# The state-space layer of a decoder trunk laid out by (set, state), with real and imaginary parts apart

## The chip, the cores and the metric

The kernel runs on one core of a Trainium2 chip. The metric is device time in microseconds (us), from one launch to its end. The kernel before took 1573.6 us (median of three runs, 1571.99 to 1575.98).

## The reference

A decoder trunk over one sequence of 512 tokens and 1024 channels: one S5 state-space layer, one layer of dilated attention, and a squared-ReLU MLP after each. The change is inside the state-space layer alone. That layer cuts the channels into 64 groups of 16; each group has 64 complex states:

```
lam_bar = exp(lam * dt)                                  # 64 groups x 64 states
b_bar   = ((lam_bar - 1) / lam)[..., None] * (b_re + i b_im)   # x 16 channels
bu      = einsum('bsgc,gpc->bsgp', u, b_bar)
state_t = lam_bar * state_(t-1) + bu_t                   # along the 512 tokens
y       = Re(einsum('bsgp,gcp->bsgc', state, c_re + i c_im)) + d * u
z       = gelu(y);  val, gate = split(z @ w_glu);  h += ada_gate * val * sigmoid(gate)
```

Everything after the layer (its GLU, the first MLP, attention, the second MLP, the final norm) is unchanged.

## The kernel before, in words

The 512 tokens are cut into 64 chunks of 8 (L = 8). Inside a chunk the recurrence is a small Toeplitz matrix per group; across chunks it is a scan over 64 steps. The groups form two sets of 32 (s = 0 and 1), and the work runs in four units (ft = 0 to 3), each with 8 groups of either set. For one unit:

- `ssm_p` (VectorE, or GpSimd for some parts): P, the input matrix of the chunk, as two products and one add (L562, L563, L564), each on 128 x 1024 elements for one set. Its argument s is the half of the unit. `ssm_p_tr` turns P with TensorE, one transpose for a group and set (L575), and ScalarE copies the result (L576). Half a unit is 8 transposes.
- `ssm_q` (GpSimd): Q, the output matrix, by three operations for each set (L590 to L592), then b_bar of the unit in its six small operations (L601 to L603, written into `bz`), then `dk`, the skip term, in two (L607).
- `ssm_k` (TensorE): the Toeplitz kernel from `bz`, Q and `dk` (L623, L626, L629); `ssm_k_copy` spreads it on ScalarE into `mt` in 16 copies (L642).
- `ssm_in_tr`/`ssm_in`: turned and modulated input; `ssm_d` (TensorE, L665): the chunk inputs; `ssm_scan` (VectorE; for the last unit the second part of it on GpSimd): rotation (L681 to L687), two scans (L690), rotation back (L700, L701) and the adds that write S (L704), four of 64 partitions because real and imaginary part lie on different partition halves than the scan's rows.
- `ssm_out` (TensorE): Toeplitz part (L718) and state part (L722); `ssm_out_tr` turns the result, applies gelu (L741), and splits it for the GLU (L744, L749).

Before the units, `ssm_params` makes the parameters: B and C arrive by DMA with the groups on partitions, TensorE turns them (L468), ScalarE copies them out in pieces with signs (L473 to L480), so that real part and imaginary part are stacked over the two halves of the partitions, for all 64 groups. `ssm_powers` turns six small matrices (L493) and builds the powers of lam_bar on VectorE and GpSimd (`cmul`, L352 to L357), each operation over 64 groups.

The order of everything in the layer is written out by hand in `ssm()`, and `pinned` keeps that order on TensorE, ScalarE, VectorE and GpSimd: each engine takes its instructions strictly in program order. Other work lies between the units: the dot products of the conditioning vector with `ada_w` (`ada_dot`, L282; `ada_steps`, L1564), whose pieces pass through the tiles `uz` and `h`, so that a piece is fetched when the dot product before has freed its tile; and `transpose_x` (L226 with ScalarE's copies L229). The GLU follows; its weights are fetched, rounded on ScalarE (L799) and their remainder made on VectorE (L801), both held by hand behind the last `ssm_k_copy` and the last scan. From there TensorE's products (L827 to L829) fill the engine. SBUF tiles of the layer come from one pool of 13 (`W`).

Of the kernel before, what the change touches and what calls it, by code (L numbers as in the profile page):

```python
# [11 lines left out]
AF = mybir.ActivationFunctionType  # L12
# [44 lines left out]
def _constants():  # L57
# [37 lines left out]
class Trunk:  # L95
# [29 lines left out]
    def setup(self):  # L125
# [4 lines left out]
        self.ones = self.cst[:, C_ONE:C_ONE + P]  # L130
# [251 lines left out]
    def ssm_params(self):  # L382
# [31 lines left out]
        q = qx[0:G, 0:12].rearrange("p (i j) n -> p i j n", j=2)  # L414
# [9 lines left out]
        nc.scalar.activation(R8, two(RD), AF.Exp, scale=float(L))  # L424
# [13 lines left out]
        v.tensor_scalar(Y8, two(X0), 4.0 / math.pi, None, ALU.mult)  # L438
# [7 lines left out]
        v.tensor_tensor(LR, two(RR), two(C0), ALU.mult)  # L446
        v.tensor_tensor(LI, two(RR), two(S0), ALU.mult)

        l1, l2 = LR[:, 0], LI[:, 0]
# [4 lines left out]
        v.tensor_tensor(CR, two(X1), two(X2), ALU.mult)  # L454
# [3 lines left out]
        v.tensor_tensor(CI, two(X1), two(X2), ALU.mult)  # L458


        bc = [self.w([P, 2, G, 16]) for _ in range(2)]
        self.bT, self.cT = bc
        for vw, o, sgn in ((bn.rearrange("g i (n c) -> g c (i n)", c=16), bc[0], ((1, 1), (-1, 1))),
                           (cn.rearrange("g c i n -> g c (i n)"), bc[1], ((1, -1), (1, 1)))):
            for hb in range(2):
                pt = self.aux_ps().rearrange("p (c g) -> p c g", g=G)
                for ch in range(8):
                    nc.tensor.transpose(pt[:, ch], vw[:, hb * 8 + ch], self.ident[0:G, 0:G])  # L468
                pv = pt.rearrange("p c g -> p g c")
                for j in range(2):  # L470
                    ov = o[:, j, :, hb * 8:hb * 8 + 8]
                    if j == 0 and sgn[j] == (1, 1):
                        nc.scalar.copy(ov, pv)  # L473
                        continue
                    for i in range(2):
                        od, pd = ov[i * 64:i * 64 + 64], pv[(i ^ j) * 64:(i ^ j) * 64 + 64]
                        if sgn[j][i] == 1:
                            nc.scalar.copy(od, pd)
                        else:
                            nc.scalar.mul(od, pd, -1.0)  # L480
        self.dn = dn
        self.q, self.qx = q, qx

    def ssm_powers(self):
# [4 lines left out]
        G = 64  # L489
        q, qx = self.q, self.qx  # L490
        pt = self.aux_ps().rearrange("p (i g) -> p i g", g=G)
        for i in range(6):
            nc.tensor.transpose(pt[:, i], q[:, i].rearrange("g s n -> g (s n)"), self.ident[0:G, 0:G])  # L493
        pw = self.w([P, 4, 8, G])
        pwr, pwi, pcr, pci = [pw[:, i] for i in range(4)]
        t1, t2, t3, t4 = [qx[:, 16 + 4 * i:20 + 4 * i] for i in range(4)]
# [7 lines left out]
        for s in range(2):  # L504
            rows = slice(s * 64, s * 64 + 64)
            v.tensor_copy(rq[rows], pt[rows, 2:4, s * GI:(s + 1) * GI])
# [12 lines left out]
        self.pw = (pwr, pwi, pcr, pci, pc0[:, 0], pc0[:, 1])  # L519
# [21 lines left out]
    def pw4(self, i, ft, s, n):  # L541
        g = s * GI + ft * 8
        return self.pw[i][:, 0:n, g:g + 8].rearrange("p l g -> p g l").unsqueeze(3).broadcast_to([P, 8, n, 16])

    def ch4(self, x, i, ft, s, n):
        g = s * GI + ft * 8
        return x[:, i, g:g + 8].unsqueeze(2).broadcast_to([P, 8, n, 16])
# [6 lines left out]
    def ssm_p(self, ft, s, eng, eng2=None):  # L554

        u = self.unit[ft]
        tz = u["zs"][:, 2 * s:2 * s + 2].rearrange("p i g c -> p (i g c)").rearrange("p (g l c) -> p g l c", g=8, c=16)
        for eng, g in ((eng, slice(0, 5)), (eng2, slice(5, 8))) if eng2 else ((eng, slice(0, 8)),):
            pp, tp = u["pp"][:, s * 8 + g.start:s * 8 + g.stop], tz[:, g]
            pr, pi, b1, b2 = [x[:, g] for x in (self.pw4(2, ft, s, 8), self.pw4(3, ft, s, 8),  # L560
                                               self.ch4(self.bT, 0, ft, s, 8), self.ch4(self.bT, 1, ft, s, 8))]
            eng.tensor_tensor(pp, pr, b1, ALU.mult)  # L562
            eng.tensor_tensor(tp, pi, b2, ALU.mult)  # L563
            eng.tensor_tensor(pp, pp, tp, ALU.add)  # L564

    def ssm_p_tr(self, ft, s):
# [5 lines left out]
        for hb in (2 * s, 2 * s + 1):  # L572
            pt = self.aux_ps().rearrange("p (g x) -> p g x", g=4)
            for j in range(4):
                nc.tensor.transpose(pt[:, j], u["pp"][:, hb * 4 + j].rearrange("p l c -> p (l c)"), self.ident)  # L575
            nc.scalar.copy(u["pT"][:, hb * 4:hb * 4 + 4], pt)  # L576

    def ssm_q(self, ft, eng):
# [6 lines left out]
        for s in range(2):  # L585
            g = s * GI + ft * 8
            g8 = slice(s * 8, s * 8 + 8)
            qs = q[:, g8, 1:8]
            tq = fl[:, 0:896].rearrange("p (g l c) -> p g l c", g=8, c=16)
            eng.tensor_tensor(qs, self.pw4(0, ft, s, 7), self.ch4(self.cT, 0, ft, s, 7), ALU.mult)  # L590
            eng.tensor_tensor(tq, self.pw4(1, ft, s, 7), self.ch4(self.cT, 1, ft, s, 7), ALU.mult)
            eng.tensor_tensor(qs, qs, tq, ALU.subtract)  # L592

        bz = u["bz"] = self.bz[ft % 2]
        for s in range(2):
            g = s * GI + ft * 8
            g8 = slice(s * 8, s * 8 + 8)
            b8 = bz[:, 0:512].rearrange("p (g x) -> p g x", x=32)[:, g8, 16:32]
            tb = fl[:, 896:1024].rearrange("p (g c) -> p g c", c=16)
            c0 = [self.pw[4 + i][:, g:g + 8].unsqueeze(2).broadcast_to([P, 8, 16]) for i in range(2)]  # L600
            eng.tensor_tensor(b8, c0[0], self.bT[:, 0, g:g + 8], ALU.mult)  # L601
            eng.tensor_tensor(tb, c0[1], self.bT[:, 1, g:g + 8], ALU.mult)
            eng.tensor_tensor(b8, b8, tb, ALU.add)  # L603
        dk = u["dk"] = self.t([32, 16, 32], "rstd", 2)
        for s in range(2):
            g = s * GI + ft * 8
            eng.tensor_tensor(dk[:, s * 8:s * 8 + 8], self.dT[:, g:g + 8].unsqueeze(2).broadcast_to([32, 8, 32]),  # L607
                              self.cst[0:32, C_DK:C_DK + 32].unsqueeze(1).broadcast_to([32, 8, 32]), ALU.mult)

    def ssm_k(self, ft):  # L610
# [1159 lines left out]
```

## Time and profile before

| what | value |
|---|---|
| median of three runs | 1573.6 us (1571.99 to 1575.98) |
| profiled execution, its own time | 1572.7 us |
| span of the profiled execution, first to last instruction | 1570.9 us |
| TensorE / VectorE / ScalarE / GpSimd busy | 1468.5 / 945.9 / 569.4 / 134.1 us |
| mean granted TensorE clock, share of full | 0.977 |

A busy time is the union of an engine's instructions. In a view in order of time, a row is a run of instructions of one line: the second number is the time from the start of the first to the end of the last, so neighbouring rows of TensorE overlap by its pipeline. In the chain of waits, rows follow each other without gaps. The text in brackets at the end of a row is idle time just before it and what ended it.

### The profile page before, as it was taken

Reading aid. Unit: us, or ns where it says so; the run is one execution under the profiler, and the core shown is the slowest. Engines: PE = TensorE matmul, PEld = TensorE weight load, DVE = VectorE, ACT = ScalarE, POOL = GpSimd, SP = SyncE. Lnnn points to the kernel's source line nnn. Section 1 sums busy time; section 2 is a strip of 40 time slices with the busy share of each in tenths; the row PEclk is TensorE's granted clock in tenths of the full one; section 3 lists DMA queues with packets and bytes.
Section 4 is the critical chain, followed back from the end, with each engine's and each line's share of the span. In section 5 each row is a group of like instructions: output and inputs, shape, how many; then the busy total and the mean of one; then the engine's idle time right before and its main releaser. Section 6 shows DMA issues by size and latency. Waiting matters only on the chain.

```text
span 1570.9 us, 27064 instructions
## 1 busy us (share of the span) xinstructions
PE 1468.5 (93%) x11540; PEld 1228.3 (78%) x11540; DVE 945.9 (60%) x1641; ACT 569.4 (36%) x989; POOL 134.1 (9%) x112
## 2 busy tenths in 40 slices
PE   2566999999999999979999999999999999999998
PEld 1445789888888888967887888798878888888887
DVE  8989996889874345657774433433558544344322
ACT  5656633424242334421332322332345423232222
POOL 8867100000000001000000000000000000000000
PEclk9888999999999999998999999999999999999999
DMA  9413581976743232354643212221325232332301
GB/s 228 133 55 82 167 236 29 323 230 196 231 143 104 85 121 88 104 164 145 180 141 102 82 55 81 82 82 55 102 84 167 78 111 82 106 99 89 107 1 54
DMA packets 214488, 188.59 MB, mean 120 GB/s; under 512 B 7480, under 2 KB 208352, under 8 KB 214368
## 3 DMA queue, kind: packets, MB, share of 16 engines
q1 hardware_dynamic: 214368, 186.87, 39.2%
q8 instruction: 90, 1.47, 0.4%
q14 instruction: 30, 0.25, 0.0%
HBM read 182.66 MB, written 4.19 MB: 119 GB/s over the span
## 4 chain that ended last, share of the span: by engine, by line
PE 73%; DVE 15%; DMA 7%; issue 3%; ACT 1%; SPq 1%; POOL 0%; DVEq 0%; ACTq 0%
PE mm L827 21%; PE mm L829 20%; PE mm L828 20%; DMA h<-in_ada_w_dram 3%; DVE aacc L1487 2%; DVE W L801 2%; DMA W<-in_attn_w_q_dram 2%; PE mm L1253 1%; PE mm L1254 1%; PE mm L1255 1%; DMA W<-in_mlp_w_dram 1%; PE mm L1170 1%; ACT W L799 1%; PE aux L1142 1%; PE aux L1107 1%
## 5 line engine op out<-in xcount | busy, mean ns | idle before, releaser
L799 ACT CAST W<-W 128x1024 fp32r<-128x1024 f32 (+1 forms) x228 | 223.4, 1030 | 400.2 <-PE mm L828 195.6
L827 PE MATMUL mm<-uz,W 128*128 128x512 f32 (+1 forms) x952 | 360.7, 381 | 3.6 <-DVE h L1383 2.7
L829 PE MATMUL mm<-uz,W 128*128 128x512 f32 (+1 forms) x952 | 358.9, 377 | 3.1 <-DVE W L801 3.1
L801 DVE TENSOR_TENSOR W<-W,W 128x1024 fp32r<-128x1024 f32 (+1 forms) x228 | 265.6, 1196 | 159.1 <-ACT W L799 137.2
L828 PE MATMUL mm<-uz,W 128*128 128x512 f32 (+1 forms) x952 | 358.3, 377 | 2.7 <-DVE uz L749 2.4
L827 PE MATMUL mm<-hid,W 128*128 128x512 f32 (+1 forms) x792 | 300.5, 380 | 0.3 <-ACT hid L1000 0.3
L828 PE MATMUL mm<-hid,W 128*128 128x512 f32 (+1 forms) x792 | 297.4, 376 | 2.5 <-DVE hid L1001 2.5
L829 PE MATMUL mm<-hid,W 128*128 128x512 f32 (+1 forms) x792 | 296.9, 375 | 0.0
L827 PEld LDWEIGHTS mm<-uz,W 128*128 128x128 f32 x952 | 180.2, 190 | 38.0 <-DVE h L1383 2.8
L829 PEld LDWEIGHTS mm<-uz,W 128*128 128x128 f32 x952 | 179.9, 189 | 36.2 <-DVE W L801 3.5
L828 PEld LDWEIGHTS mm<-uz,W 128*128 128x128 f32 x952 | 180.2, 189 | 35.2 <-DVE uz L749 2.8
L828 PEld LDWEIGHTS mm<-hid,W 128*128 128x128 f32 x792 | 150.2, 190 | 29.2 <-DVE hid L1001 3.1
L827 PEld LDWEIGHTS mm<-hid,W 128*128 128x128 f32 x792 | 149.8, 190 | 27.9 <-ACT hid L1000 0.5
L829 PEld LDWEIGHTS mm<-hid,W 128*128 128x128 f32 x792 | 149.9, 189 | 27.2
L852 DVE SCALAR_TENSOR_TENSOR h<-mm,ada,h 128x512 f32<-128x512 f32 (+1 forms) x77 | 54.1, 707 | 146.7 <-PE mm L829 146.6
L1487 DVE SCALAR_TENSOR_TENSOR aacc<-W,cs,aacc 128x256 f32<-128x256 f32 x196 | 95.5, 487 | 4.0
L1126 ACT ACTIVATE sg<-aux,st 128x192 f32<-128x192 f32 (+3 forms) x64 | 36.6, 577 | 154.5 <-DVE st L1124 148.6
L1029 DVE TENSOR_TENSOR sg<-sg 128x512 f32<-128x512 f32 x64 | 43.8, 688 | 55.3 <-ACT uz L1028 55.0
L1027 ACT ACTIVATE sg<-mm 128x512 f32<-128x512 f32 x60 | 35.6, 596 | 112.7 <-PE mm L829 108.5
L1253 PE MATMUL mm<-W,hid 128*128 128x256 f32 x256 | 73.4, 287 | 0.0
L1254 PE MATMUL mm<-W,hid 128*128 128x256 f32 x256 | 72.4, 283 | 0.0
L1255 PE MATMUL mm<-W,hid 128*128 128x256 f32 x256 | 72.4, 283 | 0.0
(329 smaller groups left out, 1699.3 us busy)
## 6 DMA issues: line engine op xcount, KB each, us to landing
W<-in_mlp_w_dram SPq DMA_DIRECT2D x64, 1024.0 KB, 5.4
W<-in_ada_w_dram SPq DMA_DIRECT2D x20, 1024.0 KB, 7.4
h<-in_ada_w_dram SPq DMA_DIRECT2D x64, 256.0 KB, 3.2
W<-in_w_kv_dram SPq DMA_DIRECT2D x12, 1024.0 KB, 5.6
W<-in_w_kv_dram SPq DMA_DIRECT2D x24, 512.0 KB, 4.2
W<-in_attn_w_q_dram SPq DMA_DIRECT2D x24, 512.0 KB, 5.7
W<-in_ssm_w_glu_dram SPq DMA_DIRECT2D x16, 512.0 KB, 5.4
W<-in_kv_ada_w_dram SPq DMA_DIRECT2D x8, 1024.0 KB, 5.6
```

The lines of the kernel that those rows point to most:

```text
L799: h = (nc.gpsimd.tensor_copy if first else nc.scalar.copy)(wh[:, ks], raw[:, ks])
L801: j = eng.tensor_tensor(wl[:, ks], raw[:, ks], wh[:, ks].bitcast(F32), ALU.subtract)
L827: nc.tensor.matmul(o, wh[:, k], uh, start=(start and k == order[0]), stop=False)
L828: nc.tensor.matmul(o, wh[:, k], ul, start=False, stop=False)
L829: self.pe_mark = nc.tensor.matmul(o, wl[:, k], uh, start=False, stop=(stop and k == order[-1])).ins
L852: self.mark = nc.vector.scalar_tensor_tensor(self.h[k][:, cs], src[:, cs], gate[:, k:k + 1], self.h[k][:, cs], ALU.mult, ALU.add).ins
L1029: nc.vector.tensor_tensor(rl, rl, rl, ALU.mult)
L1126: self.act_mark = nc.scalar.activation(p[:, 0:W], ps[:, 0:W], AF.Exp, bias=st[:, 1, e:e + 1], scale=0.125, accum_out=st[:, 2, e:e + 1]).ins
L1253: nc.tensor.matmul(ps[:, j], us[0], wh, start=(k == 0), stop=False)
L1254: nc.tensor.matmul(ps[:, j], us[0], wl, start=False, stop=False)
L1255: nc.tensor.matmul(ps[:, j], us[1], wh, start=False, stop=(k == KT - 1))
L1487: nc.vector.scalar_tensor_tensor(acc, raw[k], self.cs[:, k:k + 1], acc, ALU.mult, ALU.add)
```

## The change

Real and imaginary part are now kept as an index of the free dimension, and the two sets lie on the two halves of the partitions. `pw`, `bT`, `cT`, `pp`, `q` and `S` change their layout accordingly.

- `ssm_params`: B and C are turned part by part by plain float32 products with the identity (`by_set`), one for each channel, part and set, into 32 x 64 corners of the array; four whole copies take the place of fourteen. The parameters are no longer duplicated (`two` is gone).
- `ssm_powers`: operations over 32 groups instead of 64.
- `ssm_b_bar`: b_bar once for all units, six operations of 128 x 512 on GpSimd after the first Q; `ssm_bz` copies a unit's share into `bz` on ScalarE just ahead of `ssm_k`.
- `ssm_p`: the add is dropped; the two terms stay apart, and `ssm_p_tr` turns and adds them by two accumulating products, with the identity or its negative.
- `ssm_k`: products over 64 rows and 32 columns, the parts accumulated; `ssm_out`: state part as two products over 64 rows and 64 columns.
- `ssm_scan`: two adds of 128 partitions instead of four of 64; one scratch tile fewer.
- `dk` in one operation, `ssm_rt`'s copies of C in one; the reciprocal of `rs` ahead of the first P.

```diff
+    def by_set(self, out, x):
+        for s in range(2):
+            rows = slice(s * GI, s * GI + GI)
+            self.nc.tensor.matmul(out[s * 64:s * 64 + 64], x[rows], self.ident[rows, rows], start=True, stop=True,
+                                  tile_position=(s * GI, s * 64))
...
+        bc = self.w([P, 2, 2, GI, 16])
+        self.bT, self.cT = bc[:, 0], bc[:, 1]
+        for t, vw in enumerate((bn.rearrange("g i (n c) -> g c i n", c=16), cn)):
+            for i in range(2):
+                pt = self.aux_ps().rearrange("p (c g) -> p c g", g=GI)
+                for ch in range(16):
+                    self.by_set(pt[:, ch], vw[:, ch, i])
+                ov, pv = bc[:, t, i], pt.rearrange("p c g -> p g c")
+                if t and i:
+                    nc.scalar.mul(ov, pv, -1.0)
+                else:
+                    nc.scalar.copy(ov, pv)
...
+    def ssm_b_bar(self, eng, scratch):
+        tb = scratch[:, 0:512].rearrange("p (g c) -> p g c", c=16)
+        for i, op in enumerate((ALU.subtract, ALU.add)):
+            eng.tensor_tensor(self.bb[:, i], self.pc0[0], self.bT[:, i], ALU.mult)
+            eng.tensor_tensor(tb, self.pc0[1], self.bT[:, 1 - i], ALU.mult)
+            eng.tensor_tensor(self.bb[:, i], self.bb[:, i], tb, op)
...
             eng.tensor_tensor(pp, pr, b1, ALU.mult)
             eng.tensor_tensor(tp, pi, b2, ALU.mult)
-            eng.tensor_tensor(pp, pp, tp, ALU.add)
+        u["tp", i] = tz
...
             for j in range(4):
-                nc.tensor.transpose(pt[:, j], u["pp"][:, hb * 4 + j].rearrange("p l c -> p (l c)"), self.ident)
+                for k, (x, m) in enumerate(((u["pp"][:, hb * 4 + j], self.ident),
+                                            (u["tp", s][:, hb % 2 * 4 + j], self.ident if s else self.neg))):
+                    nc.tensor.matmul(pt[:, j], x.rearrange("p l c -> p (l c)"), m, start=(k == 0), stop=(k == 1))
...
+    def ssm_bz(self, ft):
+        bz = self.unit[ft]["bz"] = self.bz[ft % 2]
+        self.nc.scalar.copy(bz[:, 0:512].rearrange("p (i g x) -> p i g x", i=2, x=32)[:, :, :, 16:32],
+                            self.bb[:, :, ft * 8:ft * 8 + 8])
...
+            for lag in range(2):
+                for i in range(2):
+                    for q_ in (0, 2, 1, 3):
+                        m = i * 8 + j * 2 + q_ % 2
+                        z = 32 * m + (0 if lag else 16)
+                        rows = slice(q_ // 2 * 64, q_ // 2 * 64 + 64)
+                        nc.tensor.matmul(pk[q_ * 32:(q_ + 1) * 32, j, 16 * lag:], bz[rows, z:z + 32],
+                                         q[rows, m, 0:8 - lag].rearrange("p l c -> p (l c)"),
+                                         start=(lag == i == 0), stop=False, tile_position=(q_ // 2 * 64, q_ * 32))
...
-            for s in range(2):
-                rows = slice(s * 64, s * 64 + 64)
-                self.mark = v.tensor_tensor(S[i * 64:i * 64 + 64, :, s, 1:], ta[rows], tb[rows], op).ins
+            self.mark = v.tensor_tensor(ta, ta, tb, op).ins
...
-                for s in range(2):
-                    g = s * 8 + gi
-                    nc.tensor.matmul(py[s * 64:(s + 1) * 64, jj], S[:, gi, s],
-                                     q[:, g].rearrange("p l c -> p (l c)"), start=False, stop=True)
+                for i in range(2):
+                    for s in range(2):
+                        rows = slice(s * 64, s * 64 + 64)
+                        nc.tensor.matmul(py[rows, jj], S[rows, i, gi], q[rows, i * 8 + gi].rearrange("p l c -> p (l c)"),
+                                         start=False, stop=(i == 1), tile_position=(s * 64, s * 64))
...
         self.ssm_q(0, pool)
+        self.ssm_b_bar(pool, self.unit[0]["uu"][:, 1].rearrange("p g x -> p (g x)"))
+        self.nc.vector.reciprocal(self.rs, self.rs)
         self.ssm_p(0, 0, dve)
-        self.nc.vector.reciprocal(self.rs, self.rs)
...
+        self.ssm_bz(0)
         self.ssm_k(0)
...
+        self.ssm_bz(1)
         self.ssm_k(1)
...
         self.ssm_p_tr(3, 1)
         self.unit_mark = self.pe_mark
+        self.ssm_bz(2)
         self.ssm_k(2)
         self.ssm_in(3, (1,))
         self.ssm_rt(3)
         self.ssm_k_copy(2, act)
         end()
         end = self.ssm_out_tr(1)
+        self.ssm_bz(3)
         self.ssm_k(3)
 
         self.ssm_d(3)
         self.ssm_k_copy(3, act)
         self.ssm_out(2)
```

## Rows read from the trace of the kernel before

**Rows 1.** The page's 40 equal slices: busy tenths of TensorE and of VectorE.

```profile
PE   2566999999999999979999999999999999999998
DVE  8989996889874345657774433433558544344322
```

**Rows 2.** The chain of waits: start us, us, engine and line.

```profile
95.17 0.69 DVE W L681
...
154.89 0.60 DVE W L681
...
166.50 0.68 DVE W L704
...
167.30 1.90 DVE W L801 x3
169.24 0.80 PE mm L829
```

**Rows 3.** VectorE in order of time: start us, us, operation, shapes.

```profile
52.50 1.21 DVE L562 TENSOR_TENSOR W<-W,W 128x1024 f32<-128x1024 f32 x1
...
61.61 3.14 DVE L562 TENSOR_TENSOR W<-W,W 128x1024 f32<-128x1024 f32 x1
```

**Rows 4.** GpSimd in order of time.

```profile
54.82 1.79 POOL L590 TENSOR_TENSOR uz<-W,W 128x896 f32<-128x896 f32 x1 [2.37 <-PE aux L282]
...
63.60 2.80 POOL L590 TENSOR_TENSOR uz<-W,W 128x896 f32<-128x896 f32 x1
...
72.14 0.41 POOL L601 TENSOR_TENSOR bz<-W,W 128x128 f32<-128x128 f32 x1
```

**Rows 5.** TensorE in order of time, first half of the layer; "128*64" is the stationary tile.

```profile
11.80 1.97 PE L468 MATMUL aux<-cst,uz 64*128 64x64 f32 x16 [1.24 <-DMA uz<-in_ssm_c_im_dram]
...
67.23 0.85 PE L282 MATMUL aux<-uz,aacc 128*32 128x384 f32 x8 [1.79 <-DMA uz<-in_ada_w_dram]
70.37 3.40 PE L575 MATMUL aux<-cst,W 128*128 128x128 f32 x16 [2.28 <-DVE W L564]
...
84.83 0.74 PE L308 MATMUL aux<-redb,cst 128*128 128x96 f32 x2 [2.41 <-DVE redb L305]
```

**Rows 6.** TensorE in order of time, second half of the layer.

```profile
121.51 1.94 PE L575 MATMUL aux<-cst,W 128*128 128x128 f32 x8 [11.58 <-DVE sqs L653]
...
132.89 0.69 PE L718 MATMUL aux<-W,W 128*64 128x128 f32 x4 [5.89 <-DVE sg L1568]
...
138.58 0.40 PE L718 MATMUL aux<-W,W 128*64 128x128 f32 x4
...
139.12 1.10 PE L575 MATMUL aux<-cst,W 128*128 128x128 f32 x8
...
145.88 0.42 PE L623 MATMUL aux<-uz,bz 128*32 128x128 f32 x8
...
149.24 2.08 PE L665 MATMUL mm<-hid,W 128*64 128x64 f32 x64
```

**Rows 7.** The chain of waits after the layer, at a plain float32 product with 128 stationary columns.

```profile
255.81 0.79 PE aux L956 x8
```

**Rows 8.** TensorE in order of time, in the attention: a change of tile shape.

```profile
1166.78 0.67 PE L1115 MATMUL aux<-W 64*32 64x128 f32 x32
1167.38 0.50 PE L827 MATMUL aux<-uz,W 128*128 128x512 f32 x1
1167.72 0.40 PE L828 MATMUL aux<-uz,W 128*128 128x512 f32 x1
1167.96 0.40 PE L829 MATMUL aux<-uz,W 128*128 128x512 f32 x1
```

**Rows 9.** ScalarE in order of time, around the last two units.

```profile
142.53 2.50 ACT L342 ACTIVATE hid<-mm,mod 128x64 f32<-128x64 f32 x8
...
145.75 6.84 ACT L642 COPY W<-aux 32x512 f32<-32x512 f32 x16
...
154.43 1.19 ACT L744 CAST uz<-W 128x512 fp32r<-128x512 f32 x2
```

More of the change, by code (lines that the diff above doesn't have):

```diff
@@ L129, in setup @@
         self.ident = self.cst[:, C_ID:C_ID + P]
-        self.ones = self.cst[:, C_ONE:C_ONE + P]
+        self.ones = self.cst[:, C_ONE:C_ONE + 1]
+        self.neg = self.cst[:, C_NEG:C_NEG + P]
         self.swap = self.cst[:, C_SWAP:C_SWAP + P]
@@ L457, in ssm_params @@
         v.tensor_tensor(X1, X1, X3, ALU.subtract)
[L458 to L480, printed above, removed]
+        v.tensor_tensor(CI, X1, X2, ALU.mult)
+        bc = self.w([P, 2, 2, GI, 16])
[10 more added lines that the diff above has]
+                    nc.scalar.copy(ov, pv)
         self.dn = dn
         self.q, self.qx = q, qx
+    def by_set(self, out, x):
[3 more added lines that the diff above has]
+                                  tile_position=(s * GI, s * 64))
     def ssm_powers(self):
@@ L488, in ssm_powers @@
         pool = nc.gpsimd
-        G = 64
+        G = GI
         q, qx = self.q, self.qx
-        pt = self.aux_ps().rearrange("p (i g) -> p i g", g=G)
+        pt = self.aux_ps()[:, 0:6 * G].rearrange("p (i g) -> p i g", g=G)
         for i in range(6):
-            nc.tensor.transpose(pt[:, i], q[:, i].rearrange("g s n -> g (s n)"), self.ident[0:G, 0:G])
-        pw = self.w([P, 4, 8, G])
+            self.by_set(pt[:, i], q[:, i])
+        pw = self.w([P, 64, G])
+        self.bb = pw[:, 32:64].rearrange("p x g -> p (x g)").rearrange("p (i g c) -> p i g c", i=2, c=16)
+        pw = pw[:, 0:32].rearrange("p (i l) g -> p i l g", i=4)
         pwr, pwi, pcr, pci = [pw[:, i] for i in range(4)]
-        t1, t2, t3, t4 = [qx[:, 16 + 4 * i:20 + 4 * i] for i in range(4)]
+        t1, t2, t3, t4 = [qx[:, 16 + 4 * i:20 + 4 * i, 0:G] for i in range(4)]
         v.tensor_copy(pwr[:, 0], pt[:, 0])
@@ L518, in ssm_powers @@
             n *= 2
-        self.pw = (pwr, pwi, pcr, pci, pc0[:, 0], pc0[:, 1])
+        self.pw = (pwr, pwi, pcr, pci)
+        self.pc0 = [pc0[:, i].unsqueeze(2).broadcast_to([P, GI, 16]) for i in range(2)]
+    def ssm_b_bar(self, eng, scratch):
[4 more added lines that the diff above has]
+            eng.tensor_tensor(self.bb[:, i], self.bb[:, i], tb, op)
     def ssm_turns(self):
@@ L594, in ssm_q @@
[L594 to L603, printed above, removed]
@@ L604, in ssm_q @@
-        dk = u["dk"] = self.t([32, 16, 32], "rstd", 2)
[L605 to L608, printed above, removed]
+            eng.tensor_tensor(qs, self.pw4(0, ft, 7), self.ch4(self.cT, i, ft, 7), ALU.mult)
+            eng.tensor_tensor(tq, self.pw4(1, ft, 7), self.ch4(self.cT, 1 - i, ft, 7), ALU.mult)
@@ L646, in ssm_rt @@
         nc = self.nc
-        for s in range(2):
-            g = s * GI + ft * 8
-            nc.scalar.copy(self.unit[ft]["q"][:, s * 8:s * 8 + 8, 0], self.cT[:, 0, g:g + 8])
+        nc.scalar.copy(self.unit[ft]["q"].rearrange("p (i g) l c -> p i g l c", i=2)[:, :, :, 0],
+                       self.cT[:, :, ft * 8:ft * 8 + 8])
         rt = self.unit[ft]["rt"] = self.t([P, 8, NC], "sqs")
@@ L698, in ssm_scan @@
             e = eng[i]
-            ta, tb = [self.t([P, 8, NC], "sg" if e is v else "rstd", 2)[:, :, 0:n] for _ in range(2)]
+            ta = S[:, i, :, 1:]
+            tb = self.t([P, 8, NC], "sg" if e is v else "rstd", 2)[:, :, 0:n]
             e.tensor_tensor(ta, wr, a1, ALU.mult)
             e.tensor_tensor(tb, wi, b1, ALU.mult)
-            for s in range(2):
-                rows = slice(s * 64, s * 64 + 64)
-                self.mark = v.tensor_tensor(S[i * 64:i * 64 + 64, :, s, 1:], ta[rows], tb[rows], op).ins
+            self.mark = v.tensor_tensor(ta, ta, tb, op).ins
     def ssm_out(self, ft):
```

85 lines of the change are left out of this document (36 added, 49 removed).

## The prediction, made before the changed kernel was run

> **What bounds the kernel now.** I read the slices first, then the chain of waits, then each engine in order of time. In the slices [rows 1] the layer is the first four, some 160 us: VectorE is at 8 or 9 tenths, TensorE at 2 to 6; from the fifth on TensorE is full. So the layer is where VectorE counts, and what lies behind it moves as a block with the moment at which TensorE fills. The chain [rows 2] names that moment: the last scan starts at 154.89 (L681), its last add (L704) ends near 167.2, three remainders of weights (L801) follow, and at 169.24 TensorE goes on with the GLU. I forecast the shift of 169.24 and add what TensorE does more behind it.
>
> Two things must be seen beside the chain. GpSimd and VectorE hinder each other: a product of VectorE over 128 x 1024 takes 1.21 us at 52.50 and 3.14 at 61.61 [rows 3], and GpSimd's L590 1.79 alone and 2.80 against it [rows 4]; 1.21 + 1.79 is 3.0. They take turns, so in such stretches the sum of both counts. And TensorE already ends waits in places: it waits for a piece of `ada_w` at 67.23 [rows 5], and 1.94 us of transposes at 121.51 come after 11.58 us of idling [rows 6].
>
> **What goes from VectorE and GpSimd.** VectorE at 1.18 ns a column (1.21 us for 1024): P's adds, six of 1024 and one of 640, 8.0 us; the powers, 24 operations of half the width (1536 columns fewer), 1.8; S's adds, eight of sixteen at 0.68 [rows 2], 5.4. Together 15.2. GpSimd at 1.8 ns a column ((1.79 - 0.41) / 768, [rows 4]): 24 operations for b_bar at 0.41, 9.8; its adds in P, 1408 columns, 2.8; powers, 1152 columns, 2.1; half of `dk`, about 0.8. Added: six operations of 512 columns at 1.1 (from 0.41 and 1.79), 6.6, bounded by those two rows at 2.5 and 10.7. Net 8.9 less. If VectorE stayed the bound everywhere, all of it, 24 us, would be won. It doesn't stay.
>
> **Start, up to the first `ada_first` (52.50).** `by_set` needs 64 products for B and 64 for C. A float32 product leaves two records where a transpose leaves one: `ssm_d`'s 32 products are the 64 records of L665, 2.08 us [rows 6], 32 ns each with 64 stationary columns. So 256 records and 24 for the powers are 9.1 us, against 32 transposes in twice 1.97 [rows 5]. B's first ran 3.2 us before 11.80, waiting for DMA; B's real part needn't wait for the imaginary one. The end comes 0 to 3.3 us later; I take 1. Then VectorE does 1.8 + 1.2 less, GpSimd 2.1 + 2.5 + 0.8 + 2.0 less and 6.6 more, which is 3.8 less for the sum if all of it overlaps. I take -2 at 52.50 (bounds -4 and +2).
>
> **Up to the second scan (95.17).** `ssm_p_tr` of the first unit and `ada_dot` follow on TensorE. Its last piece's DMA starts when an earlier dot product frees the tile, so 67.23 moves by the same 2, and the transposes of unit 1, at 70.37 because VectorE's L564 ended then, can start near 66. There they turn from 16 records into 64, each with 128 stationary columns. The price: L956 has such products, 8 records in 0.79 us, 99 ns [rows 7]; the 16 transposes at 70.37 took 3.40, 0.2 each, and those at 139.12, in the midst of other work, some 0.12 [rows 6]: TensorE has a slow and a fast rate, and the slow one stands behind idle time. So 64 records cost 6.3 to 12.8; I take 8 (slow at first). The next fixed work, `transpose_x` paced by ScalarE, ends at 82.4 now, and VectorE is awaited until 84.83 [rows 5]. After: -4.3 + 4.6 = +0.3 on 82.4, with no wait, so L308 is 2.1 earlier. `ssm_k` may take 1 more or less. Second scan: -2.5 (bounds -7 and +3). VectorE's savings of this stretch turn into idle time ahead of L681: TensorE is the bound here.
>
> **Up to the last `ssm_in` (142.53).** From 95.17 to 121.5 VectorE is the bound now. Afterwards it needs about 20 us instead of 26, as GpSimd can't begin unit 3's Q before TensorE has used the last `ada_steps` piece, and TensorE's own row (out(0) + 2, transposes + 2.2, a wait for `bz` of 0.5) reaches the transposes of 121.51 after 20.5. So -2.5 - 5.7 = -8. From there ScalarE leads: transposes in 32 records (3.2), two copies, `mt` in 12 copies; out(1), at 132.89 because it waited for VectorE's L1568, can start 9.8 us after the transposes instead of 11.4: -9.6. Then TensorE again. out(1) took 6.2 us, mostly at the slow rate, and its last 8 records 0.54 at the fast one [rows 6]. Its state part becomes twice as many records, which should run two at a time as row tiles do: L1115's 32 records over 64 rows go in 0.60 us, 19 ns [rows 8]. But its tile shape now changes twice for each group. The first L827 after L1115 takes 0.34 us to the next instead of 0.24 [rows 8], so a change costs 0.1 and an out 1.6 more. I take 6.5 (4 to 9): +0.3. The two halves of P for unit 3 add 2.25 each (0.94 to 3.2), the copy of `bz` 0.6. L342 at 142.53 [rows 9]: -9.6 + 0.3 + 4.5 + 0.6 = -4.2.
>
> The Trainium skill, "TensorEngine Tiling (Array Packing)", section Key Properties, says that changing the tiling mode drains the engine; the 0.10 us in rows 8 agrees. It prices no drain, and without one the sum would be about 2 lower.
>
> **The new wait: `bz` of unit 3.** Now `ssm_k(3)` runs at 145.88 [rows 6], because GpSimd had written `bz` long before. After, `ssm_bz(3)` stands on ScalarE behind `ssm_k_copy(2)` and `ssm_out_tr(1)`. ScalarE has no gap from 142.53 to 155.62 [rows 9], 13.1 us, so `bz` is written 13.5 after L342, and queued behind on TensorE are `ssm_k(3)`, `ssm_d(3)`, out(2), and the scan for `ssm_d(3)`. `ssm_k`, 3.36 now, has 128 records at 19 ns and 32 small ones as now: 3.4 at the fast rate, 6 at the slow; after idling I take 4.7, then 1.3 for the first half of `ssm_d`. The scan starts 19.7 after L342; now it starts 12.4 after (154.89). That is 7.3 lost: -4.2 + 7.3 = +3.1. The scan itself is 1.6 shorter (two adds, less GpSimd): +1.5 at L801. The GLU's own need of ScalarE (L799 behind the last `mt` copy) stands no later than that.
>
> **Sum.** +1.5 at 169.24; behind it, where TensorE is full, out(3) is 2 us longer (8 groups, 16 changes, +1.6 to +3.3): +3.5, less 0.5 for products that fit into TensorE's new gap. +3 on the profiled execution: 1572.7 becomes 1575.7; the median lies 0.9 above that one, so 1576.5. `dk`, `ssm_rt` and ScalarE's fewer copies of parameters cost and bring nothing: ScalarE waits for VectorE's reciprocal there, and that comes earlier only ahead of a wait for P.
>
> **The rivals.**
> - *TensorE stays slow* (slower). Products in short bursts run at the slow rate, 0.2 us a record as at 70.37: unit 1's P +4.8, half of unit 2's +3.2, unit 3's +6.4, out(1) and k(3) +2.8, 17 in all. It decides from about 0.12 a record. For it: the slow rate at 70.37 and 132.89, both after idling. Against: the engine has more to do in between. Taken at a bit over half: 1586.
> - *Stationary load binds at the start* (slower). 16 transposes of 128 columns in 1.97 are 123 ns, 61 for 64 columns. 280 records are then 17.1 us from 8.6 at the latest, ending near 25 instead of 14.4, and all behind moves by 9 more: 1585.5. Against: L665 does 32 ns with 64 columns. The Trainium skill, "TensorE: Matmul & The Clock Gate", section LDWEIGHTS, has the load go by columns alone, at columns / 1.2 ns, 53 for 64, which would make 14.8 us of it, an estimate; L665 disagrees where column halves alternate, and `by_set` alternates them.
> - *Products are cheap* (faster). If a P record costs 54 ns, as L718's and L722's do (0.54 for 8 at 138.58, less the start of the next), the stationary load being hidden: unit 1's P -4.5, unit 2's -1.5, unit 3's -3, outs -3, k(3) -1.3: 1563. Against: L956's 99 ns.
> - *VectorE remains the bound* (faster): all 24 us, 1549.5. For it: it has 9 tenths now. Against: ScalarE's row of 13.1 us ahead of `bz(3)`, which no faster VectorE shortens.
>
> **How the numbers follow.** Chances: forecast 0.46, slow TensorE 0.18, load at the start 0.07, cheap products 0.22, VectorE 0.07. The forecast's own range is 1571 to 1582; the range for all, 1562 to 1587, leaves out VectorE's case and the ends of the others. A measurement tells 0.3% (4.7 us) from no change: below 1568.9 are the two fast cases and a little of the forecast, 0.30; above 1578.3 the two slow ones and a third of the forecast, 0.37; between, 0.33.
>
> **What would show it.** Right: L681's last run near 158, TensorE idle for about 10 us ahead of it, ended by ScalarE's copy of `bz`; 64 records for unit 1's P in about 8 us, and VectorE idle for over 5 us ahead of the second scan; TensorE's GLU going on at about 171. Wrong: P records of 54 or of 200 ns; `ssm_k(3)` not waiting; the first turn of the powers over 3 us late; VectorE without gaps up to 150.

## The result, and the profile after

The changed kernel takes 1597.3 us (median of four runs, 1593.1 to 1604.6), against 1573.2: ratio 1.0156 (95% interval 1.0115 to 1.0196), 24 us more. The forecast was 1576.5, with 1587 as the upper end. The profiled execution is the longest of the four: 1604.6 us, span 1602.8. A second series gave 1597.2 and 1.0155 (1.0136 to 1.0175), so the loss is clear of the noise.

The page's slices, TensorE and VectorE (before: [rows 1]):

```profile
PE   6886989999999999997999999999999999999998
DVE  5976785799885344667665432433457643443422
```

VectorE has come down in the layer, and TensorE has gone up to 6 to 9 tenths from the first slice on. The chain of waits (start us, us, what):

```profile
7.27 12.26 PE aux L476 x221
...
151.34 9.23 issue
...
168.26 0.69 DVE W L679
...
178.77 1.29 DVE W L798 x2
...
202.46 8.44 DMA W<-in_ssm_w_glu_dram
...
280.34 0.79 PE aux L953 x8
```

The last scan (L679, before L681) starts at 168.26 instead of 154.89 [rows 2], the remainders of weights (L798, before L801) at 178.77 instead of 167.30, and L953, which closes the GLU (before L956, 255.81 in [rows 7]), stands 24.5 later. TensorE in order of time:

```profile
63.67 7.41 PE L581 MATMUL aux<-cst,W 128*128 128x128 f32 x64
...
83.89 0.74 PE L308 MATMUL aux<-redb,cst 128*128 128x96 f32 x2 [4.15 <-DVE redb L305]
84.57 1.83 PE L623 MATMUL aux<-uz,bz 64*32 64x128 f32 x32
...
93.37 2.09 PE L663 MATMUL mm<-W,W 128*64 128x64 f32 x64
...
99.64 0.44 PE L714 MATMUL aux<-W,W 128*64 128x128 f32 x4
100.01 0.65 PE L719 MATMUL aux<-uz,W 64*64 64x128 f32 x8
100.59 0.44 PE L714 MATMUL aux<-W,W 128*64 128x128 f32 x4
...
136.39 3.84 PE L581 MATMUL aux<-cst,W 128*128 128x128 f32 x32
...
145.66 1.02 PE L623 MATMUL aux<-uz,bz 64*32 64x128 f32 x32 [0.98 <-ACT bz L606]
...
160.57 1.82 PE L623 MATMUL aux<-uz,bz 64*32 64x128 f32 x32 [9.23 <-issue]
```

The same for a group of `ssm_out` before:

```profile
100.84 0.39 PE L718 MATMUL aux<-W,W 128*64 128x128 f32 x4
...
101.28 0.39 PE L718 MATMUL aux<-W,W 128*64 128x128 f32 x4
```

A group of `ssm_out` lasts 0.95 us from L714 to the next L714, where it lasted 0.44 from L718 to the next; a record of P's sum (L581) takes 113 to 118 ns; a record of `ssm_k` (L623) 30 ns, and 57 behind idling. The loads of the stationary tiles for the same lines (PEld) are:

```profile
7.27 12.23 PEld L476 LDWEIGHTS aux<-cst,uz 32*64 32x64 f32 x222 [3.35 <-DMA uz<-in_ssm_b_re_dram]
...
93.37 1.95 PEld L663 LDWEIGHTS mm<-W,W 128*64 128x64 f32 x64 [0.41 <-issue]
...
100.00 0.41 PEld L719 LDWEIGHTS aux<-uz,W 64*64 64x64 f32 x8 [0.17 <-issue]
...
107.26 3.65 PEld L581 LDWEIGHTS aux<-cst,W 128*128 128x128 f32 x32 [0.17 <-issue]
...
145.66 0.78 PEld L623 LDWEIGHTS aux<-uz,bz 64*32 64x32 f32 x32 [1.17 <-ACT bz L606]
```

A load takes 51 to 55 ns for 64 columns, 114 for 128, 24 for 32; L663 is the exception, 64 columns in 30 ns. P's records go at the pace of their loads: with 128 moving columns, as T, the Toeplitz part of an out (L714), has them too, they take 113 to 118 ns where a record of T takes 54. `by_set` takes 55 ns with only 32 moving columns. For T and S, the state part of an out (L719), it is open whether the load or the 128 moving columns set the 54 ns, since L663 loads T's shape in 30. One reserve on `by_set`: the granted clock is given as 1.00 during it, but also from 37.35 to 43.0, where 30 records of P's sum took 5.88 us, so the level at the start is not sure. VectorE in order of time:

```profile
23.73 0.19 DVE L495 COPY W<-aux 128x32 f32<-128x32 f32 x1 [11.36 <-PE aux L476]
...
94.59 0.69 DVE L679 TENSOR_TENSOR W<-mm,hid 128x512 f32<-128x512 f32 x1 [6.58 <-PE mm L663]
...
168.26 0.69 DVE L679 TENSOR_TENSOR W<-mm,hid 128x512 f32<-128x512 f32 x1 [18.47 <-PE mm L663]
```

Its savings have become waits: 6.6 us ahead of the second scan and 18.5 ahead of the last. The 11.4 at the start are the longer `by_set`. The wait of 18.5 is the forecast new one, as ScalarE in order of time shows:

```profile
145.50 2.48 ACT L342 ACTIVATE hid<-mm,mod 128x64 f32<-128x64 f32 x8
...
150.38 6.83 ACT L641 COPY W<-aux 32x512 f32<-32x512 f32 x16 [1.60 <-PE aux L627]
...
160.06 0.41 ACT L606 COPY bz<-W 128x256 f32<-128x256 f32 x1
```

`bz(3)` (L606) stands behind the copies of `mt` (L641), and TensorE's `ssm_k(3)` starts when it is written.

Two windows, from L342 to the remainders of weights and from there to the GLU's end, give the bill of the second half. Columns: stretch, its length, TensorE's busy time and records, granted clock, DMA share and GB/s. Before:

```profile
142.53:167.30 24.77, 21.25 (x348) 0.93 0.61 171
167.30:255.81 88.51, 86.57 (x471) 0.98 0.61 179
```

After:

```profile
145.50:178.77 33.27, 23.89 (x505) 0.85 0.24 65
178.77:280.34 101.57, 95.69 (x524) 0.98 0.57 166
```

L342 is 3.0 later. The first stretch is 8.5 longer: TensorE idles 9.4 instead of 3.5 and works 2.6 more. The second is 13.1 longer: 9.1 more work, 3.9 more idling. Of the 9.1, out(3) is 4.1 (8 groups, 0.95 against 0.44), and 4.3 are products of the GLU: before, 28 records of L827 to L829 had filled TensorE's gaps ahead of 167.30; after, 9 of L824 to L826 ahead of 178.77; the other 19, each 0.227 after the last, are done behind. The first and the last of the 28 before:

```profile
151.25 0.73 PE L827 MATMUL mm<-uz,W 128*128 128x512 f32 x2
...
165.77 0.39 PE L828 MATMUL mm<-uz,W 128*128 128x512 f32 x1
```

The idling behind 178.77 is three gaps after the change:

```profile
196.44 1.09 PE L735 MATMUL aux<-cst,W 128*128 128x128 f32 x8 [1.36 <-ACT W L721]
...
206.47 0.50 PE L825 MATMUL mm<-uz,W 128*128 128x512 f32 x1 [2.32 <-DVE uz L746]
...
214.95 0.50 PE L824 MATMUL mm<-uz,W 128*128 128x512 f32 x1 [2.20 <-ACT sg L913]
```

The chain of waits runs there, up to 214.95, through the other engines and through the fetch of a GLU weight (202.46), where before it stayed on TensorE from 169.24 on. So the gap at 214.95 goes back to a late weight; whether the other two do is not shown, and no run moves these fetches alone.

### The profile page after: what moved, and what is told of

Same layout as the page of the kernel before. It is cut to its first block, busy times and chain, and to the rows that moved or that the text cites. A ratio compares the mean times of both kernels' runs of the same rounds, so it can differ in the third digit from the quotient of the medians.

```text
span 1602.8 us, 28640 instructions
## 1 busy us (share of the span) xinstructions
PE 1521.8 (95%) x12358; PEld 1272.4 (79%) x12358; DVE 923.5 (58%) x1625; ACT 564.1 (35%) x979; POOL 115.8 (7%) x88
## 4 chain that ended last, share of the span: by engine, by line
PE 79%; DVE 11%; DMA 6%; issue 2%; ACT 1%; SPq 0%; DVEq 0%; ACTq 0%
PE mm L824 21%; PE mm L825 21%; PE mm L826 21%; DMA h<-in_ada_w_dram 3%; DVE aacc L1484 3%; DVE W L798 2%; PE mm L1250 1%; PE mm L1251 1%; PE mm L1252 1%; PE aux L623 1%; DMA W<-in_attn_w_q_dram 1%; PE aux L476 1%; PE aux L581 1%; PE mm L1167 1%; PE aux L1139 1%
## 5 line engine op out<-in xcount | busy, mean ns | idle before, releaser
L824 PE MATMUL mm<-uz,W 128*128 128x512 f32 (+1 forms) x952 | 362.0, 382 | 5.8 <-DVE h L1380 2.7
L826 PE MATMUL mm<-uz,W 128*128 128x512 f32 (+1 forms) x952 | 359.1, 378 | 0.0
L798 DVE TENSOR_TENSOR W<-W,W 128x1024 fp32r<-128x1024 f32 (+1 forms) x228 | 265.5, 1196 | 162.1 <-ACT W L796 139.2
L824 PE MATMUL mm<-hid,W 128*128 128x512 f32 (+1 forms) x792 | 300.4, 380 | 0.3 <-ACT hid L997 0.3
L826 PE MATMUL mm<-hid,W 128*128 128x512 f32 (+1 forms) x792 | 296.8, 375 | 0.0
L824 PEld LDWEIGHTS mm<-uz,W 128*128 128x128 f32 x952 | 180.7, 190 | 40.0 <-DVE h L1380 2.8
L826 PEld LDWEIGHTS mm<-uz,W 128*128 128x128 f32 x952 | 180.5, 190 | 33.0
L824 PEld LDWEIGHTS mm<-hid,W 128*128 128x128 f32 x792 | 150.1, 190 | 28.0 <-ACT hid L997 0.5
L826 PEld LDWEIGHTS mm<-hid,W 128*128 128x128 f32 x792 | 149.9, 189 | 27.1
```

What stands on the lines that cost most here:

```text
L798: j = eng.tensor_tensor(wl[:, ks], raw[:, ks], wh[:, ks].bitcast(F32), ALU.subtract)
L824: nc.tensor.matmul(o, wh[:, k], uh, start=(start and k == order[0]), stop=False)
L826: self.pe_mark = nc.tensor.matmul(o, wl[:, k], uh, start=False, stop=(stop and k == order[-1])).ins
```

## Experiments

Unless it says otherwise, an edit is made on the changed kernel. Ratios are to the kernel before on the same chip, with the 95% interval.

**The wait for `bz(3)`.** `ssm_bz(3)` moved right behind `ssm_bz(2)`, ahead of L342.

```diff
         self.ssm_bz(2)
+        self.ssm_bz(3)
         self.ssm_k(2)
...
-        self.ssm_bz(3)
         self.ssm_k(3)
```

> The changed kernel with one edit: the copy of unit 3's b_bar into bz stands right behind that of unit 2, ahead of ssm_k(2), so that ScalarE's row of mt copies, gelu and casts no longer stands between it and ssm_k(3). My theory (the loss is largely this wait, and b_bar's tile, held until that copy, keeps back the third GLU weight): ssm_k(3) starts right behind the transposes of out(1), near 151.5 instead of 160.6, the last scan's L679 near 158 instead of 168.3, the third weight's DMA goes out 15 us or more earlier than 182.9; the time falls by 9 to 14 us, to 1583 to 1588. Rival (the loss is TensorE's greater number of records, and the wait only covers it): ssm_k(3) moves, but the end moves by under 4 us, to 1593 or more.

1592.3 us, 1.0113 (1.0098 to 1.0129): 5 below the first median, but the two intervals overlap. So both were run again.

> The changed kernel itself once more, beside e1_again on one chip. The first times (1597.3, ratio 1.0116 to 1.0196) and those of e1_bz_early (1592.3, 1.0098 to 1.0129) don't tell from each other by their intervals. Theory (the wait for `bz(3)` costs TensorE 9 us, of which the GLU keeps nearly all): 7 to 10 above e1_again. Rival (most of the wait is given back in the GLU and behind it): 2 to 5 above e1_again.

> The kernel of e1_bz_early once more, beside after_again: 1590 to 1593 by either theory; what tells is the distance between the two.

1597.2 and 1592.9, 1.0119 (1.0101 to 1.0137): 4.3. The windows of e1_again:

```profile
145.67:171.70 26.03, 23.23 (x504) 0.93 0.31 83
171.70:271.70 100.00, 95.82 (x525) 0.98 0.58 169
```

`ssm_k(3)` no longer waits, and the first stretch is 7.2 shorter than in the first profile of the changed kernel; the second is 1.6 shorter: the third GLU weight is fetched from 175.8 on instead of 182.9 (not 15 us earlier, as expected), and TensorE idles 4.2 instead of 5.9. By the stretches from L342 to the GLU's end (134.8, and 132.8 in after_again, against 126.0) the wait costs 7 to 9 us, by the times 4 to 5. In after_again L342 itself came 2.8 earlier than here, half of it because out(1) ran 8.2 us instead of 9.6, more of it at the fast rate; with that the GLU's ends lie 4.0 apart. Whether out(1) runs so by chance, these four profiles don't tell. By the times the rival's size holds, and the theory of 7 to 10 doesn't: the wait is a fifth of the loss.

**P's sum on TensorE.** The adds put back on VectorE and GpSimd, transposes on TensorE; alone, and together with the early `bz`.

```diff
             eng.tensor_tensor(tp, pi, b2, ALU.mult)
-        u["tp", i] = tz
+            eng.tensor_tensor(pp, pp, tp, ALU.add if i else ALU.subtract)
...
-                for k, (x, m) in enumerate(((u["pp"][:, hb * 4 + j], self.ident),
-                                            (u["tp", s][:, hb % 2 * 4 + j], self.ident if s else self.neg))):
-                    nc.tensor.matmul(pt[:, j], x.rearrange("p l c -> p (l c)"), m, start=(k == 0), stop=(k == 1))
+                nc.tensor.transpose(pt[:, j], u["pp"][:, hb * 4 + j].rearrange("p l c -> p (l c)"), self.ident)
```

> The changed kernel with one part undone: P's two terms are subtracted or added by the engine that makes them, and turned by one transpose each. By the records, a half unit goes from 32 records of 118 ns (3.8 us) to 8 (0.95), 2.8 less on TensorE each, and VectorE gets 1.2 to 3 us back for each add. My theory: behind 95 us TensorE and ScalarE lead, so the three half units in the row of units 2 and 3 (2.8 each) come off the end: 7 to 9 us less than the changed kernel, 1588 to 1590, with the wait for bz unchanged. Rival (VectorE leads there too): no gain, or up to 5 us slower.

> Both edits of the two kernels before: bz of unit 3 copied early, P's terms added by the engines. If the two losses lie one behind the other, the gains add: 17 to 22 us less than the changed kernel, 1575 to 1580. If they share one wait, the sum is no more than the larger alone: 1583 to 1588.

Alone 1606.7, 1.0209 (1.0191 to 1.0228), worse than the change; together 1589.1, 1.0100 (1.0080 to 1.0120), 3 below the early `bz` alone, which the intervals don't tell apart. Both miss what I expected. With the adds, L308 comes at 89.9 instead of 83.9: in the first half the sum on TensorE is worth 6 us. In the second it costs: in e12_both the last scan starts at 155.0, as before the change, and the remainders of weights at 167.6, though L308 came 5.7 later than with the early `bz` alone. Yet the GLU ends at 269.4, 13.7 late. So with the wait and P's sum out of the way, the rest of the loss lies behind 167, where I had allowed 1.5: 9.4 us more work of TensorE and 3.9 more idling, as in the changed kernel.

**Price of a change of tile shape.** e12_both, with Toeplitz (T) and state (S) products in the order T S S T, so that one change falls on a group instead of two.

```diff
+                parts = ("t", "s") if jj % 2 == 0 else ("s", "t")
+                for n, part in enumerate(parts):
+                    if part == "t":
...
```

> The kernel with both edits, and in ssm_out the order of Toeplitz and state part turned round for every second group, so that the tile shape changes 8 times in an out instead of 16. Records of the state part are 73 ns each in the changed kernel (0.58 for 8) and the Toeplitz ones 93 (0.37 for 4) where they were 54. If a change of shape costs 0.10 to 0.15, an out falls from 7.6 us by 0.8 to 1.2, and the time by 1 to 3 us against the kernel with both edits. If the records themselves are slow (55 ns for the load of 64 stationary columns), an out stays within 0.3 us of 7.6 and the time doesn't move.

1593.1, 1.0117 (1.0100 to 1.0134): no gain in time: 4 above e12_both, with intervals that overlap. In that run out(1) began late behind VectorE (wait of 4.4 us) and L342 stood 2.9 later than in e12_both. But its rows of TensorE give both prices (L715 is T, L721 S):

```profile
159.97 1.09 PE L721 MATMUL aux<-uz,W 64*64 64x128 f32 x16
160.99 0.66 PE L715 MATMUL aux<-W,hid 128*64 128x128 f32 x8
161.58 1.09 PE L721 MATMUL aux<-uz,W 64*64 64x128 f32 x16
```

Two groups take 1.61 instead of 1.90: a change costs 0.15. S's 16 records take (1.02 - 0.15) / 16 = 54 ns, T's 8 (0.59 - 0.15) / 8 = 55. So a record of S costs as much as one of T: the 64 x 64 tiles on the diagonal of the array gain nothing, where I had counted on two at a time.

**Is TensorE's own time paid in the second half?** The kernel before, with the outs of units 2 and 3 computed twice.

```diff
+                for _ in range(2 if ft > 1 else 1):
...
```

> The kernel before, with the products of `ssm_out` of units 2 and 3 done twice into the same bank (the second time they begin anew, so the sum is the same): 32 records of 54 ns more on each out, 3.5 us, a size like the 4.1 us that the change adds to an out, and nothing else. Theory (from L342 on TensorE is the bound and the GLU's products fill its gaps, so its own work is paid one for one): GLU's end 5.5 to 8 later, 1577 to 1580. Rival (an out lies beside ScalarE's copies and the GLU's products wait for z anyway): GLU's end less than 3 later, 1571 to 1575.

1578.0, 1.0035 (1.0021 to 1.0048): 5.5 us for 7.0 of added records. The window from L342, here 1.0 earlier, to the GLU's end:

```profile
141.57:258.71 117.14, 113.08 (x947) 0.99 0.59 171
```

117.1 us instead of 113.3: 5.2 more work, at a granted clock of 0.99 instead of 0.97, and 1.4 less idling. So in the window 3.9 of the 7.0 are paid. The GLU's end is only 2.9 later, on the rival's side of 3; another 2.6 us of the profiled execution come behind it, where nothing was changed, and only with them does the time reach the theory's range. Added work is paid by more than half, not one for one.

The same question put to the change itself, the split of `ssm_out`'s state part alone in the kernel before (e5_out_halves), has no result. What the outs cost is therefore read from the records and from the windows, and not from a run of its own.

**The start.** e1_bz_early, with C turned behind the factors of the powers.

```diff
         for i in range(6):
             self.by_set(pt[:, i], q[:, i])
+        self.ssm_bc(1)      # C; B alone stays in ssm_params
```

> The changed kernel with `ssm_bz(3)` early (as in e1_bz_early, 1592.3), and C turned behind the powers' factors instead of ahead of them: the 128 records of C leave the path to the first copy of the powers (L495). Theory (the products of `by_set` at 55 ns a record are what delays the start): L495 at 16 instead of 23.6, P's first product near 24 instead of 31.4; of these 7 us the waits for `ada_w` and ScalarE take some, 3 to 7 arrive at the second scan and at the end: 1585 to 1589. Rival (the start is covered by `ada_w`'s transfers): the second scan within 1 of 93.9, 1590 to 1593.

1583.5, 1.0073 (1.0058 to 1.0088), 0.4% less than e1_bz_early, a little more than the theory's best. VectorE in order of time:

```profile
15.82 0.19 DVE L502 COPY W<-aux 128x32 f32<-128x32 f32 x1 [3.45 <-PE aux L482]
...
31.87 0.20 DVE L1600 RECIPROCAL rs<-rs 128x8 f32<-128x8 f32 x1 [8.27 <-ACT rs L208]
```

The copy (L502, L495 before this edit) is 7.8 earlier, but P's first product is not, since the change put the reciprocal of `rs` ahead of it, and that waits for ScalarE. The gain comes later: GpSimd does the first Q from 21.6 on instead of 29.4 and has it out of VectorE's way sooner, the second P is 2.4 earlier and L308 4.8 (78.9).

**P's sum only where TensorE has room.** e6_c_behind with unit 3's P on VectorE; then the order T S S T; then the second half of unit 2 on the engines too.

```diff
+            if ft == 3:                # third run: ft * 2 + i > 4
+                eng.tensor_tensor(pp, pp, tp, ALU.add if i else ALU.subtract)
...
```

> e6_c_behind with the two terms of P of unit 3 alone added on VectorE and turned by transposes; units 0 to 2 stay on TensorE. Theory (TensorE bound from 125 on, VectorE with room there): 5.3 us less for TensorE (64 records at 118 ns against 16 transposes at about 130), 2 to 4 us more for VectorE ahead of the third scan; 3 to 5 us below e6_c_behind. Rival (VectorE or ScalarE ends the stage there): within 1.5 of e6_c_behind or above it.

> e7_p3_on_engines with the two shapes of `ssm_out` in alternating order (Toeplitz, states, states, Toeplitz), which halves the changes of shape. From the trace of e4_out_order a change costs 0.15 us and an out 6.5 instead of 7.6. Theory (TensorE paid one for one): 2 less than e7_p3_on_engines by the last two outs, 1575 to 1578. Rival (ScalarE's copies of y pace the outs, as the 3.2 us wait in e4_out_order says): the same as e7_p3_on_engines or 1 to 2 more.

> e10_order with the second half of unit 2's P added on VectorE and GpSimd too, so that five of eight halves stay on TensorE, as in e11_before_p_5_halves. There the 32 records had run at the slow rate (0.2 us); here TensorE is at work ahead of them and they run at the fast one (0.12), but VectorE waits 3.1 for them all the same (L574 at 112.71). Theory (what counts is the slow rate behind idling): no gain, within 1 of e10_order (1576.8). Rival (what counts is VectorE's wait for the half, at any rate): 2 to 3 less, 1574 to 1575.

1578.5, 1.0044 (1.0027 to 1.0061); 1576.8, 1.0023 (1.0012 to 1.0035); 1579.6, 1.0046 (1.0031 to 1.0061). The first is 4.9 below e6_c_behind, as the theory said. The second lands where its theory put it, but its interval overlaps the first's. The third lies 2.8 above e10_order, where one theory allowed 1 either way and the other wanted a gain; these intervals overlap too, so what holds is that no gain is seen. There I look at VectorE, first in e10_order, then in e13_p_5_halves:

```profile
108.36 1.22 DVE L573 TENSOR_TENSOR W<-W,W 128x1024 f32<-128x1024 f32 x1
112.71 1.36 DVE L574 TENSOR_TENSOR W<-W,W 128x1024 f32<-128x1024 f32 x1 [3.13 <-PE aux L593]
```

```profile
110.03 2.81 DVE L573 TENSOR_TENSOR W<-W,W 128x1024 f32<-128x1024 f32 x1
112.77 2.83 DVE L574 TENSOR_TENSOR W<-W,W 128x1024 f32<-128x1024 f32 x1
```

The wait for the 32 records is gone, but both products now run beside GpSimd's and last 2.8 instead of 1.2 and 1.4: the wait was no loss, since GpSimd worked alone meanwhile (its L607 took 1.80 us in e10_order and 2.79 here).

**The other way round: the kernel before with P's sum on TensorE**, for units 0 to 2, and for the first five halves.

```diff
-            eng.tensor_tensor(pp, pp, tp, ALU.add)
+            if ft == 3:                # second run: ft * 2 + s > 4
+                eng.tensor_tensor(pp, pp, tp, ALU.add)
...
+                for k, x in enumerate((u["pp"][:, hb * 4 + j], u["tp", s][:, hb % 2 * 4 + j])):
+                    nc.tensor.matmul(pt[:, j], x.rearrange("p l c -> p (l c)"), self.ident, start=(k == 0), stop=(k == 1))
```

> The kernel before with another part of the change alone: the two terms of P of units 0 to 2 added up on TensorE by two products into one PSUM bank in place of an add and a transpose; unit 3, layout, k and out as before. Theory (up to 125 VectorE is the bound, and TensorE has room): six adds less of VectorE and GpSimd, 1.2 to 3 us each; at the second scan 2 to 4 earlier, at L342 (142.53) 2 to 5 earlier, and as out and k are still cheap the end follows: 1568 to 1572. Rival (what VectorE gains TensorE loses at once, 32 records for 8 transposes): 1573 to 1577.

> e8_before_p_on_tensor with the second half of unit 2's P added on VectorE and GpSimd again, as before; the first five halves stay on TensorE. In the trace of e8_before_p_on_tensor that half's 32 records ran at the slow rate behind 11 us of idling (5.6 us for 28, 0.2 each) and VectorE waited 3.7 for them. Theory (the slow rate makes the sum on TensorE dearer than an add there): L342 1 to 3 earlier than in e8_before_p_on_tensor, 1566 to 1569. Rival (VectorE and GpSimd are the bound there and pay the add in full): 1569 to 1572.

1569.7, 0.9988 (0.9977 to 0.9998), and 1567.6, 0.9968 (0.9955 to 0.9981): the second is 5 us below the kernel before (3 to 7 by the interval), and so some 30 below the changed one. TensorE in the first:

```profile
97.12 3.84 PE L581 MATMUL aux<-cst,W 128*128 128x128 f32 x32
...
116.87 0.77 PE L581 MATMUL aux<-cst,W 128*128 128x128 f32 x2 [11.07 <-DVE W L562]
119.11 6.22 PE L581 MATMUL aux<-cst,W 128*128 128x128 f32 x30 [1.47 <-DVE sqs L659]
```

and VectorE in the same run:

```profile
125.22 1.23 DVE L562 TENSOR_TENSOR W<-W,W 128x1024 f32<-128x1024 f32 x1 [3.67 <-PE aux L581]
```

Thirty-two records take 3.84 us in the midst of work and 7.0 behind 11 us of idling, and VectorE waits for them. Without them (second run) L342 stands at 136.4 instead of 139.3, before 142.5.

## Why the prediction was wrong

Its direction was the likeliest of the three it gave, and the new wait that it forecast was there, but two terms of its sum failed: the prices of TensorE's records (1 below), and what lies behind the remainders of weights (4 below). Shifts against before, in us, by its own steps:

| step | forecast | measured |
|---|---|---|
| second P (52.50) | -2 | -3.6 |
| second scan (95.17) | -2.5 | -0.6 |
| unit 2's second transposes (121.51) | -8 | -3.8 |
| out(1) (132.89) | -9.6 | -6.1 |
| L342 (142.53) | -4.2 | +3.0 |
| last scan (154.89) | +3.1 | +13.4 |
| remainders of weights (167.30) | +1.5 | +11.5 |
| GLU's end (255.81) | +3.0 | +24.5 |
| end of the span | +3.0 | +31.9 |

At the GLU's end 21.5 us are missing from the forecast. Of these 3.5 are there when out(1) starts, 3.1 come in out(1), 0.6 up to L342, 3.1 up to the last scan, and 11.5 behind the remainders of weights; the scan gives back 0.3.

1. *The prices of TensorE's records*, the first step that failed. I priced 64 stationary columns by L665's 32 ns [rows 6], and 64 and 32 columns over 64 rows by L1115's 19 [rows 8]. Measured: `by_set` 55, S 54 and a change of shape 0.15 instead of 0.10, `ssm_k` 30 (57 slow). P's price was nearest: unit 1's 64 records took 7.4 us where I took 8. By these prices out(1) took 3.1 more than forecast, `ssm_k(3)` 1.8 and out(3) 2.1. The Trainium skill, "TensorE: Matmul & The Clock Gate", section LDWEIGHTS, makes a load columns / 1.2 ns whatever the rows: 27, 53, 107 for 32, 64, 128 columns. The rows agree at a granted clock of 1.00 (24, 51 to 55, 114), except for L663 (L665 before), 64 records in 2.09; at 0.50, from 160.57 on, `ssm_k`'s loads took 44. I had the rule as a rival for the start alone, with 7 in 100, and let that one row outweigh it. Why L663 escapes, no run here tells; `by_set` alternates the column halves as L663 does and took 55. The Trainium skill, "TensorEngine Tiling (Array Packing)", section Key Properties, says that different tiles can load and multiply in parallel; for S on the diagonal e4_out_order's 54 ns show nothing of it.

2. *From 121.51 to L342*: +0.3 + 4.5 + 0.6 forecast for out(1), P's halves and `bz`; measured 3.4 for out(1) (9.64 against 6.23) and 5.7 for the rest (9.1 from out(1)'s end to L342 against 3.4).

3. *The wait for `bz(3)`* was right in place and cause. L342 to the last scan was forecast at 19.7 and took 22.8: `bz` was written 15.0 after L342 instead of 13.5, as ScalarE waited 1.6 for `ssm_k(2)`, and `ssm_k` took 6.5 where I took 4.7. What it is worth in time, 4 to 5 us, is less than the 7.3 I gave it.

4. *Behind 169*, the second step that failed and the largest: "+2 for out(3), less 0.5". Measured +13.1, of which out(3) is 4.1, displaced products of the GLU 4.3 and idling 3.9. The step looked only at out(3), and held the GLU's products for a block behind L801. In the trace of before they already fill TensorE's gaps from 151 on, 28 of them; whatever lengthens `ssm_k`, `ssm_d` or an out there displaces them. e12_both, back in time at the remainders of weights and 13.7 late at the GLU's end, shows it; e9_out_twice shows that more than half of added work is paid there. The idling I had not thought of at all.

5. *First half*. The start's gain was right only in sum, by luck. `by_set` took 16.4 us, near the rival's 17.1, and the powers began 9.3 late, where over 3 was one of my signs of being wrong. But VectorE's powers, 20.7 us before, took 7.8, and the delay was paid back. Before:

```profile
14.45 0.23 DVE L498 COPY W<-aux 128x64 f32<-128x64 f32 x1 [1.77 <-PE aux L493]
...
35.13 1.42 DVE L562 TENSOR_TENSOR W<-W,W 128x1024 f32<-128x1024 f32 x1
```

GpSimd's Q began at 22.23 in the midst of them, and at 29.55, behind nearly all of them, after the change: of the 12.9 us, 8.1 were saved from the operation on at which Q had begun. Still the longer `by_set` was not free: e6_c_behind, without C's 128 records there, is 0.4% faster. Then b_bar on GpSimd (48.78 to 58.2) pushed its P and Q into the first scan, which lasted 20.1 us instead of 13.1. One reading was off without a consequence: L590's 1.79 us at 54.82 [rows 4] were not alone, VectorE's L564 stood beside it and took 2.81; that the two sum up holds.

The ladder of single edits, each on top of the last: 1.0155, early `bz` 1.0116 (mean of two), C behind the powers 1.0073, unit 3's P on the engines 1.0044, order of shapes 1.0023. What is left, 3.6 us, may be the outs', which are still 3 us longer each; that is argued and not shown. Behind the GLU's end the profiled execution lost another 7.4 us, after_again 3.0 and e7_p3_on_engines 0.2, so that part goes with the run and not with the change alone; its cause stays open.

## What to carry to other kernels

Before work is moved to an engine with low busy time, look at what fills its gaps in that stage: from 151 us on TensorE's were full of the GLU's products, and more than half of the added time came out behind. Price a product by its stationary load as well as by its columns: halving the rows doubled the loads here and saved nothing, so look in a trace for two such tiles that overlap before counting on it. And an edit of many parts is worth taking apart: P's sum on TensorE alone, and only where TensorE runs at its fast rate and has room, gains 0.3% in a kernel that loses 1.6% by the whole.

## What was unexpected in the hardware

- With 128 moving columns each, at a granted clock of 1.00, a record took 30 ns with 32 stationary columns (`ssm_k`), 54 with 64 (T and S) and 113 to 118 with 128 (P's sum).
- 64 x 64 tiles at opposite corners of the array, 128 moving columns: 54 ns a record, no less than a 128 x 64 tile; a change between 128 x 64 and 64 x 64: 0.15 us.
- The same sum of P took 0.12 us a record in the midst of work (granted clock 1.00, the upper of its two levels, 2.4 GHz, from 88 to 100 us in e8_before_p_on_tensor) and 0.2 us behind 11 us of idling (0.50 from 110 to 120, the lower level, 1.2 GHz).
- Powers on VectorE: 20.7 us before and 7.8 at half the width. From the operation on at which GpSimd's Q had begun it was 12.8 against 4.7; ahead of it, with GpSimd's own powers beside them both times, 7.9 against 3.0. The prediction's count by columns explains 1.8 of it.
